# The S5 layer's scan on VectorE alone, a chunk of the prompt and one of the sample in one instruction

## The chip, the cores and the metric

One core of one Trainium2 chip runs the whole kernel. Its engines are TensorE (PE in the profile; PEld its weight loads), VectorE (DVE), ScalarE (ACT), GpSimd (POOL) and SyncE (SP), which issues most DMAs. The metric is the device time of one execution in microseconds, as the median of several runs.

## What is computed

A prompt of 1024 tokens and a sample of 512 go through two layers: latent attention, which the change leaves alone, and a bidirectional S5 state space layer. Both end in a scaled residual and a layer norm. Of the reference this is the S5 layer; the scan is a linear recurrence over the tokens, in both directions, for 64 groups of 16 channels with 64 complex states each:

```python
def _s5_scan(us, lam_bar, b_bar, c):
    bu = lax.complex(jnp.einsum('lgp,gnp->lgn', us, b_bar.real),
                     jnp.einsum('lgp,gnp->lgn', us, b_bar.imag))
    a = jnp.broadcast_to(lam_bar, bu.shape)
    _, h = lax.associative_scan(_ssm_combine, (a, bu), axis=0)
    return jnp.einsum('gpn,lgn->lgp', c, h).real

def _s5(x, w_in, ...):
    u, gate = jnp.split(x @ w_in, 2, axis=-1)
    ...
    def per_seq(us):
        y_f = _s5_scan(us, lam_bar[0], b_bar[0], c[0])
        y_b = _s5_scan(us[::-1], lam_bar[1], b_bar[1], c[1])[::-1]
        return y_f + y_b

    y = lax.map(per_seq, ug).reshape(B, L, S5_WIDTH) + d.astype(f32) * uf
    y = jax.nn.gelu(y).astype(x.dtype)
    y = y * jax.nn.sigmoid(y @ w_glu + b_glu)
    return (y * jax.nn.silu(gate)) @ w_out
```

## The kernel before

Every product of full precision is three matmuls of 512 columns (`mm3`, L89 to L91) on operands cut into a high and a low part. In the S5 layer (`s5`) the tokens go in chunks of 8: 128 chunks of the prompt and 64 of the sample, 192 places. A chunk's own contribution to the state is a matmul, the recurrence over the chunks is a scan on the vector engines, and a chunk's output comes from the state ahead of it and from its own tokens (a Toeplitz matrix), again by matmuls. Partitions are (direction, state); the backward direction is stored mirrored, so that one scan does both. `X[half]` is [128, 192 places, re | im, 32 groups]; half 0 lies in the memory zone SA, half 1 in SB.

In the order of the program:

- the product that gives u (8 blocks of 128 columns, 3 chunks of 512 tokens). When u's first half is there, `states_in(q)`, q = 0 to 7, makes half 0's states, four groups each: matmuls L1203, copies L1208 and L1209 on ScalarE, L1211 and L1212 on VectorE;
- the gate's products in 14 passes (`gate(i)`): two with all three chunks of tokens, six with the first chunk alone, six with the other two. The first two passes hold `states_in(8)` to `states_in(15)`, half 1, whose copies are all ScalarE's;
- the scan: `scan` gives the three instructions of a step of one chain, a product with the factors (L1222) and two sums (L1223). The prompt's chain runs on VectorE, the sample's on GpSimd. `begin` makes a chain ready, `advance(n)` emits n steps of each ready chain in turn. Half 0 is one chain of 32 groups; half 1 is two of 16 groups, which begin in the first and in the second gate pass;
- in the last six passes `first(i)` puts the outputs of four groups, i = 0 to 9, between the gate's products: `states_out(i)` gathers the states of four groups (L1343 on VectorE, L1344 on ScalarE, L1345 on GpSimd) into one place, which all i below 10 share with each other, `outputs(i)` makes 12 matmuls (L1359 to L1361), the gelu (L1363) and, after every second i, writes 128 rows of y (L1367);
- the gated linear unit (GLU): `load_y(m)` fetches row block m of y (L1403) into a place that the gate's weights held, GpSimd rounds it to the high part (L1406), VectorE subtracts (L1407); `load_w` does the same with weights (L1419 to L1421). `early(kt)` multiplies row block kt for the first two column blocks. The outputs 10 to 15 stand between;
- the rest of the GLU, the output projection and the norm.

The Tile layer's scheduler takes this program and settles the order on every engine by its own simulated timeline, so an engine's order differs from the program's. The scan's and the copies' code:

```python
1214    def scan(chain, c):
1216        half, lo, hi, seq = chain
1217        eng = (nc.vector, nc.gpsimd)[seq]
1218        prev, cur = (X[half][:, 128 * seq + i, :, lo:hi] for i in (c - 1, c))
1219        sh = [128, 2, 2, hi - lo]
1220        lam = k.lam[:, :, :, half * 32 + lo:half * 32 + hi]
1221        t = k.scan[half][seq][:, :, :, lo:hi]
1222        return [lambda: eng.tensor_mul(t, prev.unsqueeze(2).broadcast_to(sh), lam),
1223                lambda: eng.tensor_add(cur, cur, t[:, 0]), lambda: eng.tensor_add(cur, cur, t[:, 1])]
...
1232    def advance(n):
1234        for _ in range(n):
1235            for f in zip(*[scan(h, todo[h].pop(0)) for h in todo if todo[h]]):
1236                for g in f:
1237                    g()
...
1343        nc.vector.tensor_copy(st[0:64], xv[0:64])
1344        nc.scalar.copy(st[64:128, :, :, 0:128], xv[64:128, :, :, 127::-1])
1345        nc.gpsimd.tensor_scalar(st[64:128, :, :, 128:192], xv[64:128, :, :, 191:127:-1], 1.0, 0.0, op0=ALU.mult, op1=ALU.add)
```

In tile names, `ident` is half 0's buffer for the prompt's products (the identity is no longer needed then), `scan` the other two, `lam` the factors.

## Time and profile before

| | |
|---|---|
| median of 3 runs | 1690.88 us (1687.87 to 1691.36) |
| span of the profiled execution | 1688.0 us |
| TensorE busy | 1571.6 us, 93% |
| VectorE busy | 1177.9 us, 70% |
| GpSimd busy | 630.6 us, 37% |
| ScalarE busy | 571.1 us, 34% |

The span runs from the first instruction to the last; for the profiled execution the page has no other time. A busy share is a mean over all stages of the program, and says little of the one stage that the change is in. A matmul's end is modelled, so its price is read from the distance of one start to the next. In rows of the order of time, "x2" merges two instructions, and the square bracket gives the idle time ahead of an instruction with what ended it. The names of waits are the last releaser by the profile.

### The profile page before, as it was taken

Reading aid. Unit: us, or ns where it says so; the run is one execution under the profiler, and the core shown is the slowest. Engines: PE = TensorE matmul, PEld = TensorE weight load, DVE = VectorE, ACT = ScalarE, POOL = GpSimd, SP = SyncE. Lnnn points to the kernel's source line nnn. Section 1 sums busy time; section 2 is a strip of 40 time slices with the busy share of each in tenths; the row PEclk is TensorE's granted clock in tenths of the full one; section 3 lists DMA queues with packets and bytes.
Section 4 is the critical chain, followed back from the end, with each engine's and each line's share of the span. In section 5 each row is a group of like instructions: output and inputs, shape, how many; then the busy total and the mean of one; then the engine's idle time right before and its main releaser. Section 6 shows DMA issues by size and latency. Waiting matters only on the chain.

```text
span 1688.0 us, 23831 instructions
## 1 busy us (share of the span) xinstructions
PE 1571.6 (93%) x7932; PEld 1332.1 (79%) x7932; DVE 1177.9 (70%) x2667; ACT 571.1 (34%) x997; POOL 630.6 (37%) x1137
## 2 busy tenths in 40 slices
PE   8997777999999999999999999999877899999997
PEld 7996566887887878888888888888656788887886
DVE  5539995377766676788757742489999975553776
ACT  3442222153444444444511113416613363222000
POOL 6807673133232232344311000077798624233110
PEclk9998988999999999999999999999988999999999
DMA  5654555923223232442344426525665589564553
GB/s 172 176 158 148 168 197 159 324 67 88 77 77 102 67 98 86 148 138 80 122 150 141 125 94 177 152 49 145 195 185 163 174 260 296 187 206 142 187 143 93
DMA packets 205930, 249.68 MB, mean 148 GB/s; under 512 B 26608, under 2 KB 149104, under 8 KB 204784
## 3 DMA queue, kind: packets, MB, share of 16 engines
q1 hardware_dynamic: 197168, 232.36, 45.9%
q10 hardware_dynamic: 8640, 15.80, 2.6%
q8 instruction: 63, 1.03, 0.3%
q14 instruction: 59, 0.48, 0.1%
HBM read 155.89 MB, written 90.11 MB: 146 GB/s over the span
## 4 chain that ended last, share of the span: by engine, by line
PE 62%; DVE 26%; DMA 6%; issue 2%; POOL 2%; ACT 1%; SPq 1%; DVEq 0%; POOLq 0%; ACTq 0%
PE B L90 8%; PE B L91 8%; PE S L91 8%; PE B L89 8%; PE S L89 8%; PE S L90 8%; DVE SA L1223 4%; DVE SB L1223 4%; PE B L538 4%; DVE ident L1222 3%; DMA X<-SG 2%; DVE scan L1222 2%; PE S L504 2%; PE S L503 2%; DVE SA L1071 2%
## 5 line engine op out<-in xcount | busy, mean ns | idle before, releaser
L523 POOL TENSOR_SCALAR SC<-SC,R 128x1024 f32<-128x1024 f32 (+1 forms) x96 | 99.8, 1040 | 226.7 <-DVE R L522 189.8
L89 PE MATMUL B<-X,SB 128*128 128x512 f32 x392 | 156.7, 400 | 2.1 <-DVE SC L1125 1.5
L90 PE MATMUL B<-X,SB 128*128 128x512 f32 x392 | 154.8, 395 | 0.0
L91 PE MATMUL B<-X,SB 128*128 128x512 f32 x392 | 154.5, 394 | 0.0
L540 ACT CAST X<-B 128x512 fp32r<-128x512 f32 x160 | 89.9, 590 | 128.2 <-PE B L538 127.9
L541 DVE TENSOR_TENSOR X<-B,X 128x512 fp32r<-128x512 f32 x160 | 106.3, 684 | 23.4 <-ACT X L540 23.0
L516 ACT ACTIVATE SC<-S,R 128x1024 f32<-128x1024 f32 (+1 forms) x96 | 93.8, 977 | 66.3 <-DVE R L513 59.1
L513 DVE TENSOR_REDUCE R<-S 128x1 f32<-128x1024 f32 (+1 forms) x96 | 99.3, 1039 | 21.5 <-PE S L504 21.1
L1223 DVE TENSOR_TENSOR SB<-SB,scan 128x32 f32<-128x32 f32 x504 | 101.2, 236 | 2.1
L538 PE MATMUL B<-ident,SC 128*128 128x128 f32 x640 | 89.5, 272 | 5.9 <-POOL SC L523 5.9
L538 PEld LDWEIGHTS B<-ident,SC 128*128 128x128 f32 x640 | 76.4, 140 | 21.2 <-POOL SC L523 6.8
L89 PEld LDWEIGHTS B<-X,SB 128*128 128x128 f32 x392 | 74.8, 191 | 17.4 <-DVE SC L1125 1.7
L91 PEld LDWEIGHTS B<-X,SB 128*128 128x128 f32 x392 | 74.6, 190 | 15.6
L90 PEld LDWEIGHTS B<-X,SB 128*128 128x128 f32 x392 | 74.8, 191 | 14.8
L1223 DVE TENSOR_TENSOR SA<-SA,ident 128x64 f32<-128x64 f32 x252 | 80.9, 321 | 4.9
L89 PE MATMUL B<-X,R 128*128 128x512 f32 x192 | 78.7, 410 | 5.3 <-ACT R L1323 3.0
L90 PE MATMUL B<-X,R 128*128 128x512 f32 x192 | 76.3, 397 | 0.0
L91 PE MATMUL B<-X,R 128*128 128x512 f32 x192 | 75.6, 395 | 0.0
L89 PE MATMUL S<-SA,X 128*128 128x384 f32 (+2 forms) x208 | 69.5, 342 | 6.4 <-POOL SA L96 6.4
L90 PE MATMUL S<-SA,X 128*128 128x384 f32 (+2 forms) x208 | 70.3, 340 | 0.3 <-DVE SA L97 0.3
L91 PE MATMUL S<-SA,X 128*128 128x384 f32 (+2 forms) x208 | 69.6, 335 | 0.0
L99 POOL TENSOR_SCALAR R<-R,gq 128x64 fp32r<-128x64 f32 (+1 forms) x96 | 35.7, 383 | 89.1 <-PE B L90 45.9
(414 smaller groups left out, 4549.2 us busy)
## 6 DMA issues: line engine op xcount, KB each, us to landing
R<-WG SPq DMA_DIRECT2D x112, 128.0 KB, 3.4
R<-EU SPq DMA_DIRECT2D x52, 224.0 KB, 3.3
EU<-SA SPq DMA_DIRECT2D x16, 512.0 KB, 4.3
WO<-SA SPq DMA_DIRECT2D x8, 1024.0 KB, 4.1
WG<-X SPq DMA_DIRECT2D x16, 512.0 KB, 3.0
X<-WO SPq DMA_DIRECT2D x16, 512.0 KB, 6.2
SG<-SC ACTq DMA_DIRECT2D x24, 256.0 KB, 2.5
SC<-SG SPq DMA_DIRECT2D x24, 256.0 KB, 2.9
```

The costliest lines, as they stand in the source:

```text
L89: nc.tensor.matmul(ps, ah, bh, start=first, stop=False)
L90: nc.tensor.matmul(ps, ah, bl, start=False, stop=False)
L91: nc.tensor.matmul(ps, al, bh, start=False, stop=last)
L99: nc.gpsimd.tensor_scalar(hi, raw, g, 0.0, op0=ALU.mult, op1=ALU.add)
L513: nc.vector.reduce_max(nm, self.S[:, :L], axis=AX.X, negate=True)
L516: nc.scalar.activation(P, self.S[:, :L], AF.Exp, bias=nm, accum_out=rsum)
L523: nc.gpsimd.tensor_scalar(P, P, rsum, 0.0, op0=ALU.mult, op1=ALU.add)
L538: nc.tensor.transpose(ps[:, t, :], P[:, (t0 + t) * 128:(t0 + t + 1) * 128], self.k.ident)
L540: nc.scalar.copy(a[:, :, qsl], ps)
L541: nc.vector.tensor_sub(b[:, :, qsl], ps, a[:, :, qsl])
L1222: return [lambda: eng.tensor_mul(t, prev.unsqueeze(2).broadcast_to(sh), lam), lambda: eng.tensor_add(cur, cur, t[:, 0]), lambda: eng.tenso ...
L1223: lambda: eng.tensor_add(cur, cur, t[:, 0]), lambda: eng.tensor_add(cur, cur, t[:, 1])]
```

## The change

The scan runs on VectorE alone. For places below 64 one instruction covers chunk c of the prompt and chunk c of the sample (places c and 128 + c): a product of 128x256 and two sums of 128x128. Above 64 only the prompt is left: 128x128 and 128x64 while the other half is in turn with it, and two chains of 16 groups when a half is alone. Half 1 becomes one chain of 32 groups, which begins when all its states are emitted. `advance` is given a time in us instead of a number of steps. The mirrored copy of the sample's states goes from GpSimd to ScalarE. The product buffers are tiles of their own, and the factors are laid out by half. The size of a scratch buffer for DMAs that GpSimd describes is set; none of the kernel's DMAs is of that kind (the queues in the profile are the two hardware ones). The rest of the diff takes out comments.

```diff
-    def scan(chain, c):
-        half, lo, hi, seq = chain
-        eng = (nc.vector, nc.gpsimd)[seq]
...
-    def begin(half, lo, hi):
-        for seq, n in enumerate((128, 64)):
-            todo[half, lo, hi, seq] = list(range(2, n))
...
+    todo = [[], []]
+
+    def step(half, c, lo=0, hi=32):
+        n = hi - lo
+        if c < 64:
+            both = X[half][:, 0:192].rearrange("p (a b) r g -> p a b (r g)", b=64)[:, 0:3:2]
+            prev, cur = both[:, :, c - 1], both[:, :, c]
+            sh = [128, 2, 2, 64]
+            lam = k.lam[:, half].rearrange("p k r g -> p k (r g)").unsqueeze(1).broadcast_to(sh)
+            t = k.scan[half]
+            return [lambda: nc.vector.tensor_mul(t, prev.unsqueeze(2).broadcast_to(sh), lam),
+                    lambda: nc.vector.tensor_add(cur, cur, t[:, :, 0]), lambda: nc.vector.tensor_add(cur, cur, t[:, :, 1])]
+        prev, cur = (X[half][:, i, :, lo:hi] for i in (c - 1, c))
+        lam = k.lam[:, half, :, :, lo:hi]
+        t = k.scan[half][:, 0].rearrange("p k (r g) -> p k r g", r=2)[:, :, :, lo:hi]
+        return [lambda: nc.vector.tensor_mul(t, prev.unsqueeze(1).broadcast_to([128, 2, 2, n]), lam),
+                lambda: nc.vector.tensor_add(cur, cur, t[:, 0]), lambda: nc.vector.tensor_add(cur, cur, t[:, 1])]
+
+    def begin(half):
+        todo[half] = list(range(2, 128))
+        owed[0] = min(owed[0], 0.0)
+
+    owed = [0.0]
+
+    def advance(us):
+        owed[0] += us
+        while owed[0] > 0 and any(todo):
+            ready = [h for h in range(2) if todo[h]]
+            if len(ready) == 1 and todo[ready[0]][0] >= 64:
+                h, c = ready[0], todo[ready[0]].pop(0)
+                steps = [step(h, c, 0, 16), step(h, c, 16, 32)]
+                owed[0] -= 0.72
+            else:
+                cs = [todo[h].pop(0) for h in ready]
+                steps = [step(h, c) for h, c in zip(ready, cs)]
+                owed[0] -= 1.15 if len(ready) == 1 else sum(0.74 if c < 64 else 0.48 for c in cs)
+            for f in zip(*steps):
                 for g in f:
                     g()
...
-            advance(6)
+            advance(5.5)
...
-            if (i, kt) == (0, 6):
-                begin(1, 0, 16)
-            elif (i, kt) == (1, 6):
-                begin(1, 16, 32)
+            if (i, kt) == (1, 6):
+                begin(1)
...
-            advance(5 if i == 0 else (2, 2, 1, 1)[4 - len(cs)] if len(cs) == 3 else 1)
+            advance(0.69 * len(cs) + (1.4 if i < 2 else 0))
...
-        nc.gpsimd.tensor_scalar(st[64:128, :, :, 128:192], xv[64:128, :, :, 191:127:-1], 1.0, 0.0, op0=ALU.mult, op1=ALU.add)
+        nc.scalar.copy(st[64:128, :, :, 128:192], xv[64:128, :, :, 191:127:-1])
...
     def first(i):
-        while i == 8 and any(todo.values()):
-            advance(1)
+        if i == 8:
+            advance(1e3)
         outputs(i, states_out(i))
+        advance(1.3)
         load(i + 2)
...
-    while any(todo.values()):
-        advance(1)
+    advance(1e3)
...
-        k.scan = [(t[0], t[2]), (t[1], t[2])]
+        k.lam = const.tile([128, 2, 2, 2, G // 2], F32, name="lam")
+        k.scan = [const.tile([128, 2, 2, G], F32, name="scan%d" % i) for i in range(2)]
```

In the lines of the kernel after, a combined step is L1226 and L1227, a step of the prompt alone L1231 and L1232, the copies of the states are L1361 to L1363, the output matmuls L1377 to L1379, the subtraction for y L1425.

The order of VectorE where half 1's first step stands. Before, with half 0's own steps around it (SA is half 0, SB half 1):

```order
L1222 TENSOR_TENSOR ident<-SA,lam 128x128 [waits DVE_49]
L1223 TENSOR_TENSOR SA<-SA,ident 128x64 [waits DVE_49] x2
L1222 TENSOR_TENSOR scan_80<-SB,lam 128x4x16 [waits Activation_49]
L1222 TENSOR_TENSOR ident<-SA,lam 128x128 [waits DVE_49]
L1223 TENSOR_TENSOR SB<-SB,scan_80 128x2x16 [waits DMAHW3_49,DMAHW4_49,DMAHW2_49,DMAHW5_49,DMAHW1_49,DMAHW6_49,DMAHW0_49,DMAHW7_49,DVE_49,PE_49]
L1223 TENSOR_TENSOR SA<-SA,ident 128x64 [waits DVE_49]
```
and now:

```order
L1231 TENSOR_TENSOR scan_80<-SA,lam 128x4x16 [waits DVE_49] x2
L1232 TENSOR_TENSOR SA<-SA,scan_80 128x2x16 [waits DVE_49] x4
L1231 TENSOR_TENSOR scan_80<-SA,lam 128x4x16 [waits DVE_49] x2
L1232 TENSOR_TENSOR SA<-SA,scan_80 128x2x16 [waits DVE_49]
L1226 TENSOR_TENSOR scan_81<-SB,lam 128x256 [waits Activation_49]
L1232 TENSOR_TENSOR SA<-SA,scan_80 128x2x16 [waits DVE_49] x2
L1227 TENSOR_TENSOR SB<-SB,scan_81 128x2x64 [waits DMAHW3_49,DMAHW4_49,DMAHW2_49,DMAHW5_49,DMAHW1_49,DMAHW6_49,DMAHW0_49,DMAHW7_49,DVE_49,PE_49]
L1232 TENSOR_TENSOR SA<-SA,scan_80 128x2x16 [waits DVE_49]
```
Before, half 1's first instruction waits for ScalarE's copies of the first 16 groups, q = 8 to 11; now for those of all 32. The second sum's rows show that half 0's prompt steps go on between. Ahead of the place stand, of half 0, 62 combined steps and 26 rounds of two chains of 16; behind it 27 such rounds and 11 whole steps, in turn with 39 of half 1, up to the first L1361.

The order of TensorE at the first output product (L1359 before, L1377 now; X and R are the gate's operands in L89 to L91). Before:

```order
L1359 MATMUL B<-X_11015 128x192 x2
L1360 MATMUL B<-X_11016,X_11015 128x192
L1361 MATMUL B<-X_11016,X_11015 128x192
L1359 MATMUL B<-X_11015 128x192
L1360 MATMUL B<-X_11016,X_11015 128x192
```
and now:

```order
L1377 MATMUL B<-X_10370 128x192 x2
L89 MATMUL B<-X_88,R 128x512
L90 MATMUL B<-X_89,R 128x512
L91 MATMUL B<-X_88,R 128x512
L89 MATMUL B<-X_90,R 128x512
```
The other ten matmuls of output 0 followed its first two directly, and 30 gate matmuls stood between outputs 0 and 1. Now 60 gate matmuls stand there, and then the rest of output 0 and all of output 1 without any between; outputs 2 to 7 have 24 gate matmuls ahead of each. After the gate's last matmul come two matmuls of output 9, 24 of the GLU with y0 and y1, the rest of output 8, and 24 more with y2 and y3. Before, output 8 stood among the gate's matmuls and outputs 9 to 12 ahead of all of the GLU.

The order of VectorE at the scan's end (L1407 and L1425 are the subtractions for y, L1421 and L1439 those for the weights). Before:

```order
L1222 TENSOR_TENSOR scan_80<-SB,lam 128x4x16 [waits DVE_49]
L1223 TENSOR_TENSOR SB<-SB,scan_80 128x2x16 [waits DVE_49] x2
L1343 COPY X_12057<-SB 64x1536 [waits PE_49]
L1421 TENSOR_TENSOR X_12059<-X_12057,X_12059 128x512 [waits DMAHW3_49,PE_49,Activation_49]
L1343 COPY X_11016<-SB 64x1536 [waits PE_49]
L1421 TENSOR_TENSOR X_12059<-X_12057,X_12059 128x512 [waits DMAHW1_49,Activation_49]
L1343 COPY X_12057<-SB 64x1536 [waits DVE_49,PE_49,Pool_49]
L1343 COPY X_12057<-SB 64x1536 [waits DVE_49,PE_49]
L1407 TENSOR_TENSOR X_12059<-R,X_12059 128x1536 [waits DMAHW5_49,Pool_49]
```
and now:

```order
L1231 TENSOR_TENSOR scan_81<-SB,lam 128x4x16 [waits DVE_49]
L1425 TENSOR_TENSOR X_11474<-R,X_11474 128x1536 [waits DMAHW7_49,Pool_49]
L1231 TENSOR_TENSOR scan_81<-SB,lam 128x4x16 [waits DVE_49]
L1232 TENSOR_TENSOR SB<-SB,scan_81 128x2x16 [waits DVE_49] x2
L1439 TENSOR_TENSOR X_11473<-X_11472,X_11473 128x512 [waits DMAHW1_49,Activation_49]
L1232 TENSOR_TENSOR SB<-SB,scan_81 128x2x16 [waits DVE_49]
L1425 TENSOR_TENSOR X_11474<-R,X_11474 128x1536 [waits DMAHW0_49,Pool_49]
L1232 TENSOR_TENSOR SB<-SB,scan_81 128x2x16 [waits DVE_49]
L1361 COPY X_10371<-SB 64x1536 [waits DVE_49]
L1361 COPY X_11472<-SB 64x1536
```
The whole scan stood ahead of the first subtraction for y. Now the last steps stand behind that for y0 (the first L1425), and the copy of output 8's states, the first L1361 here, behind that for y1. On SyncE the load of y7 stood behind four loads of weights that came after the last rows of y were written; now it follows the writes, with three such loads behind it.

## Rows read from the trace of the kernel before

**Rows 1.** Order of time on PE; start us, us, line, operation, tiles [idle before]

```profile
1249.85 0.39 PE L89 MATMUL B<-X,R 128*128 128x512 f32 x1
...
1251.21 0.49 PE L1359 MATMUL B<-X 128*128 128x192 f32 x2
...
1263.16 0.98 PE L1360 MATMUL B<-X,X 128*128 128x192 f32 x2 [11.14 <-DVE scan L1222]
...
1379.26 0.48 PE L1359 MATMUL B<-X 128*128 128x192 f32 x2
...
1379.58 0.49 PE L1360 MATMUL B<-X 128*128 128x192 f32 x2
...
1454.18 0.39 PE L89 MATMUL B<-X,X 128*128 128x512 f32 x1
```

**Rows 2.** Busy time by stage; us, busy us (instructions) by engine, granted clock, DMA

```profile
core 0: us, PE busy (x) PEld busy (x) DVE busy (x) ACT busy (x) POOL busy (x), PEclk, DMA share, GB/s
1249.85:1454.18 204.33, 169.46 (x806) 149.61 (x804) 163.57 (x635) 78.18 (x82) 115.04 (x243) 0.92 0.66 206
```

**Rows 3.** Waits of PE in the stretch; us in total, times, longest

```profile
PE B L1360 <- DVE scan L1222: 19.6, 2, 11.1
...
PE B L1359 <- DMA X<-TT: 3.6, 1, 3.6
```

**Rows 4.** The copies of the states; the last row, of the line's answer: min/median/max ns

```profile
1241.79 19.81 POOL L1345 TENSOR_SCALAR X<-SA 64x512 f32<-64x512 f32 x1 [3.32 <-PE B L90]
...
1260.39 2.06 ACT L1344 COPY X<-SA 64x1024 f32<-64x1024 f32 x1 [17.90 <-DVE SA L1223]
...
L1343 DVE COPY X<-SA x8: 1445/1552/2475, 1260.4 to 1355.3; 64x1536 f32<-64x1536 f32 x8
```

**Rows 5.** Order of time on DVE, half 0's steps beside GpSimd's

```profile
1102.50 0.43 DVE L1222 TENSOR_TENSOR ident<-SA,lam 128x128 f32<-128x128 f32 x1
...
1103.84 0.43 DVE L1222 TENSOR_TENSOR ident<-SA,lam 128x128 f32<-128x128 f32 x1
```

**Rows 6.** The same, GpSimd without work

```profile
1146.52 0.29 DVE L1222 TENSOR_TENSOR ident<-SA,lam 128x128 f32<-128x128 f32 x1
...
1147.36 0.29 DVE L1222 TENSOR_TENSOR ident<-SA,lam 128x128 f32<-128x128 f32 x1
```

**Rows 7.** The same, three chains in turn

```profile
1248.80 0.22 DVE L1222 TENSOR_TENSOR scan<-SB,lam 128x64 f32<-128x64 f32 x1
1248.93 0.29 DVE L1222 TENSOR_TENSOR ident<-SA,lam 128x128 f32<-128x128 f32 x1
1249.13 0.22 DVE L1222 TENSOR_TENSOR scan<-SB,lam 128x64 f32<-128x64 f32 x1
```

**Rows 8.** The same, half 1's two chains alone

```profile
1298.25 0.54 DVE L1223 TENSOR_TENSOR SB<-SB,scan 128x32 f32<-128x32 f32 x4
...
1298.98 0.54 DVE L1223 TENSOR_TENSOR SB<-SB,scan 128x32 f32<-128x32 f32 x4
```

**Rows 9.** Order of time on ACT, the last states of half 1

```profile
1209.78 1.05 ACT L1211 COPY SB<-S 64x508 f32<-64x508 f32 x1
1210.63 0.64 ACT L1212 COPY SB<-S 64x252 f32<-64x252 f32 x1
```

**Rows 10.** The eight loads of y, L1403

```profile
DMA to landing us min/median/max: 4.5/6.3/7.3
```

**Rows 11.** The way of y7: gelu, load, rounding, subtraction

```profile
1423.68 0.49 ACT L1363 ACTIVATE X<-B 128x384 f32<-128x384 f32 x1 [1.46 <-PE B L1361]
...
1434.19 0.34 SPq L1403 DMA_DIRECT2D R<-Y  x1
...
1440.21 0.43 SPq L1403 DMA_DIRECT2D R<-Y  x1
...
1446.94 1.48 POOL L1406 TENSOR_SCALAR X<-R 128x1536 fp32r<-128x1536 f32 x1 [4.98 <-DMA R<-Y]
...
1448.46 1.76 DVE L1407 TENSOR_TENSOR X<-R,X 128x1536 fp32r<-128x1536 f32 x1 [3.27 <-POOL X L1406]
```

More of the change, by code (lines that the diff above doesn't have):

```diff
@@ L1009, in prep_a @@
         for r in range(2):
-            nc.gpsimd.tensor_copy(lam[:, r, r], pr[:, 8, :])
-            nc.gpsimd.tensor_scalar(lam[:, 1 - r, r], pi[:, 8, :], (1.0, -1.0)[r], 0.0, op0=ALU.mult, op1=ALU.add)
+            halves = [x[:, 8, :].rearrange("p (h g) -> p h g", h=2) for x in (pr, pi)]
+            nc.gpsimd.tensor_copy(lam[:, :, r, r], halves[0])
+            nc.gpsimd.tensor_scalar(lam[:, :, 1 - r, r], halves[1], (1.0, -1.0)[r], 0.0, op0=ALU.mult, op1=ALU.add)
         self.pb = [self.t("pbr", [128, T, G]), self.t("pbi", [128, T, G])]
@@ L1212, in states_in @@
             cp(x[64:128, :, :, 129:192], v[64:128, :, :, 191:128:-1])
-    def scan(chain, c):
-        half, lo, hi, seq = chain
-        eng = (nc.vector, nc.gpsimd)[seq]
-        prev, cur = (X[half][:, 128 * seq + i, :, lo:hi] for i in (c - 1, c))
-        sh = [128, 2, 2, hi - lo]
-        lam = k.lam[:, :, :, half * 32 + lo:half * 32 + hi]
-        t = k.scan[half][seq][:, :, :, lo:hi]
-        return [lambda: eng.tensor_mul(t, prev.unsqueeze(2).broadcast_to(sh), lam),
-                lambda: eng.tensor_add(cur, cur, t[:, 0]), lambda: eng.tensor_add(cur, cur, t[:, 1])]
@@ L1225, in s5 @@
-    todo = {}
-    def begin(half, lo, hi):
-        for seq, n in enumerate((128, 64)):
-            todo[half, lo, hi, seq] = list(range(2, n))
-    def advance(n):
-        for _ in range(n):
-            for f in zip(*[scan(h, todo[h].pop(0)) for h in todo if todo[h]]):
+    todo = [[], []]
[14 more added lines that the diff above has]
+                lambda: nc.vector.tensor_add(cur, cur, t[:, 0]), lambda: nc.vector.tensor_add(cur, cur, t[:, 1])]
@@ L1271, in s5 @@
                     if q == 7:
-                        begin(0, 0, 32)
+                        begin(0)
             ps = ahead.get((m, c))
@@ L1581, in trunk @@
             setattr(k, n, const.tile(shape, F32, name=n))
-        k.lam = const.tile([128, 2, 2, G], F32, name="lam")
-        t = [k.ident] + [const.tile([128, 128], F32, name="scan%d" % i) for i in range(2)]
-        t = [x.rearrange("p (k r g) -> p k r g", k=2, r=2) for x in t]
-        k.scan = [(t[0], t[2]), (t[1], t[2])]
+        k.lam = const.tile([128, 2, 2, 2, G // 2], F32, name="lam")
+        k.scan = [const.tile([128, 2, 2, G], F32, name="scan%d" % i) for i in range(2)]
         k.bcol = const.tile([128, 8], F32, name="bcol")
@@ L1647 @@
     from concourse.bass_utils import run_bass_kernel_spmd
-    nc = bacc.Bacc("TRN2", target_bir_lowering=False, num_devices=1)
+    nc = bacc.Bacc("TRN2", target_bir_lowering=False, num_devices=1, dynamic_dma_scratch_size=1024)
     ins = arrays(inputs)
```

## The prediction

> **What bounds the kernel now.** I read the busy times by stage first, then TensorE's waits, then VectorE's order of time in the scan, then the way of y into the gated linear unit (GLU). Everything before 1101 us stays as it is: the scan starts there, and the order of TensorE up to its first output product is the same in both kernels. From there I compare one stretch, between two matmuls that both orders have: from 1249.85 us, seven matmuls ahead of the first output product, to the first product with y7 at 1454.18 us; after it the two orders of TensorE are equal again. In this stretch the order has 420 matmuls of 512 columns and 192 output matmuls, in both kernels. A 512-column matmul takes 0.227 us (six from 1249.85 to 1251.21), an output matmul 0.325 us; the trace shows it as two instructions [rows 1]. So the work is 420 x 0.2268 + 192 x 0.325 = 157.7 us, and the stretch lasts 204.3 us, of which TensorE is busy 169.5 [rows 2]. It loses 46.6 us: 34.9 us idle and 11.8 us in running slower than those two prices, at a granted clock of 0.92 in the mean [rows 2], so part of the time at the lower of its two levels, 1.2 GHz instead of 2.4. This is all that the change can win here.
>
> Who causes the idle time: the output products wait 19.6 us in two waits, 11.1 the longest, each for a VectorE instruction of the scan, and 3.6 us for a load of the Toeplitz matrices [rows 3]. The longest ends at 1263.16 [rows 1]: the states of the first four groups could be copied only when half 0's scan was done, which ScalarE's copy had awaited until 1260.39 [rows 4]. So VectorE's scan bounds this stretch, and TensorE's products are its victims.
>
> **What a scan step costs on VectorE.** Beside GpSimd's sample chain a step of half 0 (a 128x128 product, two 128x64 sums) repeats every 1.34 us [rows 5]. The same step without GpSimd at work repeats every 0.84 us [rows 6]; each of its three instructions waits for the one before. With three chains in turn nothing waits: a 128x64 product gives way to the next after 0.13 us, a 128x128 after 0.20 [rows 7], so 64 more columns cost 0.067 us. Two chains of 16 groups in turn need 0.73 us a round [rows 8].
>
> The combined step (product 128x256, sums 128x128) is in no row. Lower bound: no more than today's solo step, 0.84. Upper bound: the sample's step as a second full step behind it, 1.68. I take 0.84 plus four times 0.067 (two blocks of 64 columns in the product, one in each sum) = 1.11 us alone, and 0.34 + 2 x 0.20 = 0.74 us beside another chain, since rows 7 already show that columns cost their count and no more. A prompt-only step of 32 groups beside another chain is 0.20 + 2 x 0.13 = 0.47.
>
> **Half 0.** 62 combined steps, 68.8 us, then 26 split rounds, 18.9: from 1101.4 to about 1189. Then VectorE meets the first instruction of half 1 in its queue, which waits for ScalarE; the other 38 prompt steps of half 0 are queued behind it. ScalarE's last copy of half 1's states ends at 1211.3 [rows 9]; so VectorE stands still some 22 us. Before, the first of two half-1 chains could begin earlier. Behind it: 39 half-1 steps at 0.74, 27 split rounds at 0.67, 11 steps at 0.47 = 52.1 us, half 0 done at 1263.4. That is 3 us later than today's, not earlier.
>
> **Outputs 0 to 7.** What is won comes from the order on TensorE: ahead of output 0 stand 60 more gate matmuls (13.6 us), which today come after it. TensorE reaches output 0 at 1249.85 + 0.65 + 13.6 = 1264.1. The states' copies then take VectorE 1.55 us and ScalarE 2.06 [rows 4]; the wait is about 2 us where 11.1 stood. Output 1 follows with nothing between, and its states have the same place: ScalarE copies 2.06 and now also the sample's 64x512, bounded by the nearest copy, 64x508 in 1.05 [rows 9], so TensorE waits 3.3 us. The six after that have 24 gate matmuls each ahead (5.4 us) against 3.1 us on ScalarE and, on VectorE, 7 solo steps (7.8 us) and a copy against 9.3 us: no wait, but hardly any slack. Up to the gate's end the order has 252 gate matmuls and 100 output matmuls: 1249.85 + 57.2 + 32.5 + 5.3 = 1344.8, and a few us more of slow running, against 1379.26 today [rows 1].
>
> **From the gate's end G to y7.** Now something else is late. The place of y0's rows is freed only at G. A load of y lands in 6.3 us [rows 10], GpSimd rounds it in 1.48, VectorE subtracts in 1.76 [rows 11]: with the handovers 9.9 us. The order has 24 products with y0 and y1 ahead of output 8, and the last scan steps of VectorE stand behind y0's subtraction: TensorE idles about 9.4 us. y2's rows come into the place of y0's, so y2 is ready some 10.3 us behind y0, and TensorE has 5.4 + 3.2 us of products until then: 1.7 us; output 11's load, as today, 3.6 [rows 3]. y6 and y7: from an output's gelu, the rows are stored, read back, rounded and subtracted. Today this took from 1424.2 to 1450.2 us, 26 us, and the load went out only at 1440.2, behind four weight loads; the load of another row block ahead of them went out at 1434.2 [rows 11]. The change moves them behind y7's load, which saves up to these 6 us: 20. TensorE has 78 products, 17.7 us, after output 15: I count the difference, some 2.5 us, for y6 and y7 together (both ends: nothing, if the queue is empty; 8.3 us, if all stays as today).
>
> **The sum.** Idle: 2 + 3.3 + 9.4 + 1.7 + 3.6 + 2.5 = 22.5 us instead of 34.9. Slow running in proportion, 11.8 x 22.5/34.9 = 7.6. Loss 30.1 instead of 46.6: **16.5 us** won. The profiled span of 1688.0 becomes 1671.5. The median of the runs, 1690.88, stands 2.9 us above the span, so I say 1674. GpSimd's own work goes at no cost elsewhere: its scan and copies had nothing behind them that TensorE waits for, except the clash with VectorE, which is in the 1.34 against 0.84.
>
> GpSimd's mirrored copy at 1241.79 took 19.81 us [rows 4], and within this time VectorE's instructions kept their distances of 0.13 and 0.20 us [rows 7]: the copy starved, not VectorE. The Trainium skill ("SBUF — State Buffer", section "SBUF: two separate sides") says that the two engines' shared port pair is an exclusive lock, held for the whole instruction by whoever comes first. By that rule moving eight copies of 1.1 us off GpSimd would free VectorE of 9 us more before output 7, and the sum would be 9 us better. The trace disagrees at this copy, though the step's 1.34 against 0.84 shows the clash in the other direction.
>
> **Rivals.**
> 1. *VectorE becomes the bound (slower).* It is busy 163.6 of the stretch's 204.3 us today [rows 2], and takes over all that GpSimd did in the scan. If a combined step costs x more than my 1.11 (two pieces of memory in one operand), the first 62x hide in the 22 us of standing still, up to x = 0.36; the 39 steps before output 0 and the 23 between outputs do not: 62x. The gain is gone at x = 0.27, and it is slower by over 0.2% from 0.32, a step of 1.43 us; at the bound 1.68 the time would be 1674 + 35 + 13 = 1722. For it: no row has such an operand. Against it: VectorE's states' copy reads 1536 scattered elements in 1.55 us at the median [rows 4], so scattered columns cost no more. The Trainium skill ("Perfetto Trace Analysis", section "Optimizing Scalar/DVE Operations") advises to take work off a saturated VectorE, even to GpSimd, though it doubts that between these two. The trace bears out the doubt.
> 2. *The tail of y stays as slow as today (smaller gain).* 26 us against 17.7 us of products: 8.3 us idle instead of 2.5, and the slow running after it, 8 us in all: 1682. For it: the queue of DMAs is as full. Against it: the weight loads go behind.
> 3. *TensorE is covered better (larger gain).* If y0's load lands in 4.5 us, the shortest of the eight [rows 10], output 0 and the tail don't wait: idle 12, slow 4, loss 16: 30 us won, 1660.
> 4. *Nothing is won.* Half 0 isn't done earlier, and TensorE loses at GLU what it wins before: 1690. This needs 35 us of idle time again, 12 us more than the rows give.
>
> **Chances.** Forecast 0.61 (1665 to 1682); rival 1 0.11, of which 0.10 over 0.2% slower; rival 2 0.13; rival 3 0.09; rival 4 0.06. About 0.2%, 3.4 us, is what a measurement of this kernel tells from no change: faster 0.83, same 0.07, slower 0.10. Range 1658 to 1688: it takes in rivals 2 and 3 and leaves out the others.
>
> **What the profile would show.** Right: combined steps every 1.11 us from 1101; VectorE idle some 20 us before 1211, ended by ScalarE; output 0's wait near 2 us at 1264 to 1267; the gate ending near 1346; one wait near 9 us for y0 then. Wrong: steps over 1.3 us; half 0 done after 1275; waits of over 3 us at outputs 2 to 7; over 6 us idle ahead of y6 or y7.

## The result, and the profile after

| | before | after |
|---|---|---|
| median of the runs | 1688.04 us (5 runs, 1687.31 to 1691.36) | 1676.96 us (5 runs, 1674.56 to 1681.59) |
| ratio | | 0.9932, 95% interval 0.9915 to 0.9950 |
| span of the profiled execution | 1688.0 us | 1675.1 us |

The change wins 11.1 us at the medians and 12.9 us between the two profiled executions. The forecast was 16.5 us.

The stretch of the prediction, from the first output product (1249.54) to the first product with y7 (now 1443.19), by the windows view; from 1353.90 on TensorE waits for y0. It answers to [rows 2] and holds the same number of matmul instructions (806).

```profile
core 0: us, PE busy (x) PEld busy (x) DVE busy (x) ACT busy (x) POOL busy (x), PEclk, DMA share, GB/s
1249.54:1353.90 104.36, 96.71 (x453) 82.34 (x452) 89.41 (x481) 50.35 (x53) 0.00 (x0) 0.97 0.70 210
1353.90:1443.19 89.29, 72.12 (x353) 62.36 (x353) 41.89 (x82) 36.30 (x40) 17.28 (x10) 0.92 0.70 226
1249.54:1443.19 193.65, 168.83 (x806) 144.70 (x805) 131.30 (x563) 86.64 (x93) 17.28 (x10) 0.95 0.70 217
```

The stretch is 193.65 us long instead of 204.33. TensorE is idle for 24.8 us of it (34.9 before) and runs slow for 168.83 - 157.66 = 11.2 us (157.66 is the work at full price that the prediction gives as 157.7; 11.8 before). VectorE is busy 131.3 us instead of 163.6, although it does GpSimd's part too. So the stretch wins 10.7 us. Behind it, from y7 to the end, the execution is 1.9 us shorter (TensorE was idle there for 1.6 us before and is not now), and ahead of it 0.3 us.

What TensorE waits for in the stretch, by the waits view (us in total, times, longest); beside [rows 3]:

```profile
PE S L89 <- POOL X L1424: 11.7, 1, 11.7
PE B L1378 <- ACT X L1363: 3.5, 1, 3.5
PE B L1378 <- DMA X<-WO: 1.8, 1, 1.8
PE B L1378 <- ACT X L1362: 1.8, 1, 1.8
PE B L1377 <- ACT X L1381: 1.4, 1, 1.4
PE B L1377 <- ACT R L1341: 1.1, 1, 1.1
```

The 19.6 us for the scan are gone. Instead there is one wait of 11.7 us for y0, and small ones for ScalarE's copies of the states. In TensorE's order of time the waits stand here (the bracket is the idle time ahead), beside [rows 1]:

```profile
1268.28 1.01 PE L1378 MATMUL B<-X,X 128*128 128x192 f32 x2 [1.76 <-ACT X L1362]
...
1276.84 0.59 PE L1378 MATMUL B<-X 128*128 128x192 f32 x2 [3.50 <-ACT X L1363]
...
1351.17 0.39 PE L91 MATMUL B<-X,R 128*128 128x512 f32 x1
...
1353.27 0.59 PE L1377 MATMUL B<-X 128*128 128x192 f32 x2 [1.12 <-ACT R L1341]
1365.55 0.80 PE L89 MATMUL S<-X 128*128 128x512 f32 x1 [11.68 <-POOL X L1424]
```

Output 0 waits 1.8 us where 11.1 stood, output 1 3.5; the gate's last product is at 1351.17 instead of 1379.03 (the output product behind it stands in [rows 1]); then comes y0's wait.

VectorE's order of time: two combined steps at the scan's start, beside [rows 5], and the standstill in front of half 1, with the end of half 0.

```profile
1100.68 0.43 DVE L1226 TENSOR_TENSOR scan<-SA,lam 128x256 f32<-128x256 f32 x1
1101.14 0.62 DVE L1227 TENSOR_TENSOR SA<-SA,scan 128x128 f32<-128x128 f32 x2
1101.79 0.42 DVE L1226 TENSOR_TENSOR scan<-SA,lam 128x256 f32<-128x256 f32 x1
...
1211.47 0.42 DVE L1226 TENSOR_TENSOR scan<-SB,lam 128x256 f32<-128x256 f32 x1 [23.28 <-ACT SB L1213]
...
1264.23 1.53 DVE L1361 COPY X<-SA 64x1536 f32<-64x1536 f32 x1
...
1371.30 1.54 DVE L1361 COPY X<-SB 64x1536 f32<-64x1536 f32 x1
```

A combined step takes 1.11 us. VectorE stands still 23.3 us, half 0 is done at 1264.2, and the first states of half 1 are copied only at 1371.3, when the whole scan is over. That this copy stands so late was in the order listed with the change, but the prediction did not ask what it costs; the experiments turn on it.

### The profile page after: what moved, and what is told of

Same layout as the page of the kernel before. It is cut to its first block, busy times and chain, and to the rows that moved or that the text cites. A ratio compares the mean times of both kernels' runs of the same rounds, so it can differ in the third digit from the quotient of the medians.

```text
span 1675.1 us, 23206 instructions
## 1 busy us (share of the span) xinstructions
PE 1574.3 (94%) x7932; PEld 1330.7 (79%) x7932; DVE 1121.1 (67%) x2640; ACT 581.4 (35%) x1009; POOL 415.4 (25%) x563
## 4 chain that ended last, share of the span: by engine, by line
PE 72%; DVE 14%; DMA 8%; ACT 2%; issue 2%; POOL 1%; SPq 1%; DVEq 0%; ACTq 0%; POOLq 0%
PE B L89 11%; PE B L90 11%; PE B L91 11%; PE S L91 9%; PE S L89 9%; PE S L90 9%; PE B L538 4%; DVE SA L1072 2%; PE S L1204 2%; PE S L504 2%; PE S L503 2%; DVE SA L1070 2%; DVE R L1071 2%; DVE SA L1227 1%; DMA R<-WG 1%
## 5 line engine op out<-in xcount | busy, mean ns | idle before, releaser
L89 PE MATMUL B<-X,SB 128*128 128x512 f32 x392 | 156.6, 399 | 2.4 <-DVE SC L1126 1.5
L91 PE MATMUL B<-X,SB 128*128 128x512 f32 x392 | 154.3, 394 | 0.0
L89 PEld LDWEIGHTS B<-X,SB 128*128 128x128 f32 x392 | 74.9, 191 | 17.7 <-DVE SC L1126 1.7
L91 PEld LDWEIGHTS B<-X,SB 128*128 128x128 f32 x392 | 74.5, 190 | 15.6
L89 PE MATMUL B<-X,R 128*128 128x512 f32 x192 | 79.0, 412 | 5.7 <-ACT R L1341 3.0
L91 PE MATMUL B<-X,R 128*128 128x512 f32 x192 | 76.3, 398 | 0.0
L89 PE MATMUL S<-SA,X 128*128 128x384 f32 (+2 forms) x208 | 70.4, 344 | 5.5 <-POOL SA L96 5.5
L91 PE MATMUL S<-SA,X 128*128 128x384 f32 (+2 forms) x208 | 69.9, 337 | 0.0
L90 PE MATMUL B<-X,X 128*128 128x512 f32 x168 | 68.2, 406 | 0.3 <-DVE X L541 0.2
L89 PE MATMUL B<-X,X 128*128 128x512 f32 x168 | 67.3, 401 | 0.0
L91 PE MATMUL B<-X,X 128*128 128x512 f32 x168 | 66.2, 394 | 0.0
```

The lines of the kernel that those rows point to most:

```text
L89: nc.tensor.matmul(ps, ah, bh, start=first, stop=False)
L90: nc.tensor.matmul(ps, ah, bl, start=False, stop=False)
L91: nc.tensor.matmul(ps, al, bh, start=False, stop=last)
```

## The experiments

Two questions: why y0's wait is there, and which part of the change earns the gain. Every run was compared with the kernel before on the same chip; the medians:

| kernel | median us | ratio, 95% interval |
|---|---|---|
| the change | 1676.96 | 0.9932 (0.9915 to 0.9950) |
| y0_piece | 1675.76 | 0.9922 (0.9903 to 0.9941) |
| copy_on_gpsimd | 1678.38 | 0.9935 (0.9917 to 0.9953) |
| before_copy_on_scalar | 1685.18 | 0.9974 (0.9962 to 0.9986) |
| before_scan_on_vector | 1667.91 | 0.9888 (0.9866 to 0.9911) |
| scan_only | 1672.31 | 0.9914 (0.9898 to 0.9929) |
| unmerged | 1676.47 | 0.9929 (0.9915 to 0.9943) |
| late_begin | 1673.41 | 0.9901 (0.9883 to 0.9919) |
| copies_on_vector | 1672.31 | 0.9906 (0.9889 to 0.9924) |
| scan_and_copies_on_vector | 1680.66 | 0.9951 (0.9936 to 0.9967) |
| scan_and_two_copies_on_vector | 1669.03 | 0.9878 (0.9860 to 0.9896) |
| unmerged_one_chain | 1685.22 | 0.9975 (0.9966 to 0.9985) |

**y0's place.** The rows of y0 get a place of their own, cut off from those that the gate's results pass through, so that their load need not wait until the gate's last result is stored.

```diff
-    ry = Region(k, "R", (13, F32))
+    ry = Region(k, "R", (6, F32), (7, F32))
```

> The changed kernel, with the place of y0's rows cut off from the places that the gate's results pass through. Theory: in the changed kernel y0's load goes out only at 1359.1 us because its place is one piece with that of the gate's last result, whose store to memory must land first; with a piece of its own the load needs only the gate's last matmul (1351.4) and goes out near 1354, TensorE's wait for y0 falls from 11.7 us to about 7, and the time by 4 to 6 us, to about 1672. Rival: the wait is set by the weights' load or by VectorE's scan steps ahead of y0's subtraction, and the time stays at 1677 within 2 us.

Not so: 1675.76 us, which can't be told from the change. SyncE's and GpSimd's order of time, first of the change, then of this kernel:

```profile
1359.11 0.79 SPq L1421 DMA_DIRECT2D R<-Y  x2
...
1364.02 4.59 POOL L1424 TENSOR_SCALAR X<-R 128x1536 fp32r<-128x1536 f32 x2 [217.26 <-DMA R<-Y]
```

```profile
1355.45 3.86 SPq L1421 DMA_DIRECT2D R<-Y  x2
...
1362.46 3.00 POOL L1424 TENSOR_SCALAR X<-R 128x1536 fp32r<-128x1536 f32 x2 [213.74 <-DMA R<-Y]
...
1367.98 0.80 PE L90 MATMUL S<-X 128*128 128x512 f32 x1 [3.20 <-DVE X L1425]
...
1355.00:1364.00 9.00, 0.01 (x1) 0.01 (x1) 7.05 (x44) 0.62 (x1) 1.48 (x2) 0.55 0.97 353
```

The load goes out 3.7 us earlier and its rounding starts only 1.6 us earlier: the DMA engines are 97% busy in these 9 us (last row, the windows view). The wait for y0's high part shrinks by 1.0 us, but the one for its low part, VectorE's subtraction, grows from 1.0 to 3.2: scan steps stand ahead of the subtraction on VectorE, and it starts only at 1366.2. So the rival holds. The place alone is not the bound; behind it stand the load, which shares the DMA engines with the output's and the GLU's weights, and VectorE's scan.

**The copy back on GpSimd.** The change, but with the mirrored copy of the sample's states where it was.

```diff
-        nc.scalar.copy(st[64:128, :, :, 128:192], xv[64:128, :, :, 191:127:-1])
+        nc.gpsimd.tensor_scalar(st[64:128, :, :, 128:192], xv[64:128, :, :, 191:127:-1], 1.0, 0.0, op0=ALU.mult, op1=ALU.add)
```

> The changed kernel, with the copy of the sample's mirrored states back on GpSimd: one part undone. Theory: beside VectorE steps that wait for each other the copy takes 1.1 to 2.7 us and runs next to ScalarE's, so the wait ahead of output 1 falls from 3.5 us to about 2.4 and the time by 0 to 2 us. Rival 1: where VectorE's split rounds leave no gap the copy starves as the one of 19.8 us did, outputs 4 to 8 wait 5 us or more each, and the time is above 1690. Rival 2, by the rule of the exclusive port pair: each copy stops VectorE for 1.1 us, 16 copies, 1 to 3 us slower.

1678.38 us: no difference from the change. Output 1 waits 2.7 us instead of 3.5, and other waits take up the rest.

**The copy alone.** The kernel before, with only this line the other way round (copy on ScalarE, sample's scan still on GpSimd).

> The kernel before, with only the copy of the sample's mirrored states moved from GpSimd to ScalarE: one part alone. Theory: the starved copy of 19.8 us ended before VectorE's own copy, so it delayed nothing; the time stays within 3 us of 1688. Rival, by the rule of the exclusive port pair: VectorE gains 8 copies of 1.1 us ahead of output 7 and the time falls by about 9 us, to 1679.

1685.18 us, 3.5 less than before: about the theory's 3, and far from the rival's 9. TensorE's waits and the stretch by windows:

```profile
PE B L1360 <- ACT X L1344: 30.2, 1, 30.2
...
1247.42:1449.33 201.91, 163.99 (x805) 144.71 (x805) 156.07 (x684) 91.86 (x97) 65.60 (x185) 0.92 0.67 209
```

The order came out differently: one wait of 30.2 us at output 0 instead of the waits of 11, 8, 5 and 3 us. TensorE is idle for longer than before (201.91 - 163.99 = 37.9 us instead of 34.9), but runs slow for only 163.99 - 157.7 = 6.3 us instead of 11.8. So slow running does not follow the idle time. And since the order changed too, the copy's effect is not seen by itself.

**The scan's engine and the copy, nothing merged.** The kernel before with two lines changed; the sample's chain is now one more chain on VectorE, in turn with the prompt's, and half 1 stays two chains of 16 groups.

```diff
-        eng = (nc.vector, nc.gpsimd)[seq]
+        eng = nc.vector
...
-        nc.gpsimd.tensor_scalar(st[64:128, :, :, 128:192], xv[64:128, :, :, 191:127:-1], 1.0, 0.0, op0=ALU.mult, op1=ALU.add)
+        nc.scalar.copy(st[64:128, :, :, 128:192], xv[64:128, :, :, 191:127:-1])
```

> The kernel before, with the scan's sample chains on VectorE but as instructions of their own, half 1 still in two chains that begin early, and the copy on ScalarE: the change without merging. Theory: what pays is that GpSimd no longer slows VectorE (1.34 against 0.84 us a step) and what the new order on TensorE hides; two chains in turn fill each other's waits, so half 0 costs 0.94 us for a step of prompt and sample against 1.115 merged; half 0 done near 1265 us, the time 1670 to 1682, no slower than the changed kernel. Rival: merging is what makes the scan fit on VectorE; without it VectorE has some 42 us more to issue, ends the scan later than 1385 us, and the time is 1700 or more.

1667.91 us: the change's own idea in two lines, 2 us below the theory's range, and faster than the change by 9 us at the medians, 7 by the ratios; the two intervals don't touch. VectorE's order of time: a step of half 0, the two standstills, the states of half 1; and the copies of half 0's states, of the line's answer.

```profile
1101.83 0.29 DVE L1222 TENSOR_TENSOR ident<-SA,lam 128x128 f32<-128x128 f32 x1
1102.04 0.29 DVE L1222 TENSOR_TENSOR scan<-SA,lam 128x128 f32<-128x128 f32 x1
...
1102.78 0.28 DVE L1222 TENSOR_TENSOR ident<-SA,lam 128x128 f32<-128x128 f32 x1
...
1176.94 0.23 DVE L1222 TENSOR_TENSOR scan<-SB,lam 128x64 f32<-128x64 f32 x1 [11.07 <-ACT SB L1211]
...
1211.26 0.23 DVE L1222 TENSOR_TENSOR scan<-SB,lam 128x64 f32<-128x64 f32 x1 [4.51 <-ACT SB L1211]
...
1343.88 1.55 DVE L1343 COPY X<-SB 64x1536 f32<-64x1536 f32 x1
...
1373.13 0.42 DVE L1223 TENSOR_TENSOR SB<-SB,scan 128x32 f32<-128x32 f32 x2
...
L1343 DVE COPY X<-SA x8: 1446/1539/1556, 1270.6 to 1331.9; 64x1536 f32<-64x1536 f32 x8
```

Four things are seen. Six small instructions, two chains in turn, take 0.95 us for the same work as the merged step's three in 1.11: nothing waits for the instruction before it. The first chain of half 1 begins at 1176.9, 34.5 us before half 1 begins in the change. The scan's end, 1373.5, is no earlier than the change's, but states of half 1 are copied from 1343.9 on: its first 16 groups are done long before the others. So outputs 8 to 11 can stand ahead of y0, and y0's wait is gone. And half 0 is not done sooner: its first copy is 10 us later than before (1260.4, [rows 4]), but the eight follow one another faster, and the last is at 1331.9 instead of 1355.3. What TensorE waits for there:

```profile
PE B L1360 <- DVE SB L1223: 10.9, 2, 7.4
PE B L1360 <- ACT X L1344: 3.5, 1, 3.5
PE B L1359 <- DMA X<-TT: 2.3, 1, 2.3
```

**The scan's engine alone.** As above with the copy left on GpSimd.

> The kernel before with one line changed: all chains of the scan on VectorE; the mirrored copy of the sample's states stays on GpSimd, nothing is merged. Together with the runs that moved the copy alone (1685.2) and both (1667.9) this gives the parts of the gain. Theory (the scan's two engines taking turns at memory is what cost): nearly all of the 20 us comes from the scan: 1668 to 1673 us, with waits of at most a few us for the GpSimd copy. Rival (the GpSimd copy, starved by a VectorE that now never pauses, needs some 20 us for each of eight blocks): TensorE waits for it at output 0 and again at outputs 1 to 7, 1680 us or more.

1672.31 us: the theory. Of the 20 us between before and the unmerged kernel some 16 come with the scan's engine; the copy's 4 more are at the edge of what these intervals tell apart. The scheduler settles a new order for each of these kernels, so the 16 us are those of the engine together with the order that follows; no run holds the order fixed. GpSimd's copies and VectorE's sums in their order of time:

```profile
1241.83 29.83 POOL L1345 TENSOR_SCALAR X<-SA 64x512 f32<-64x512 f32 x1 [93.05 <-DVE ident L1222]
...
1296.54 1.18 POOL L1345 TENSOR_SCALAR X<-SA 64x512 f32<-64x512 f32 x1 [6.58 <-PE B L1361]
...
1295.40 0.48 DVE L1223 TENSOR_TENSOR SB<-SB,scan 128x32 f32<-128x32 f32 x4
...
1296.42 1.45 DVE L1223 TENSOR_TENSOR SB<-SB,scan 128x32 f32<-128x32 f32 x4
```

The first copy starves for 29.8 us, as in [rows 4]. The other seven of half 0 do not: each takes some 1.1 to 2.6 us, and VectorE's instructions beside it lose about 1 us (here 0.48 becomes 1.45).

**The change without its merged instruction.** Loops, turns and the one chain of half 1 as in the change.

```diff
-                steps = [step(h, c) for h, c in zip(ready, cs)]
+                steps = [step(h, c, seq=q) for h, c in zip(ready, cs) for q in range(2 if c < 64 else 1)]
```

> The changed kernel with its loop structure kept, but the sample's step again as three instructions of its own, taking turns with the prompt's (no 128x256 product). The scheduler answers by finishing half 0 ahead of half 1's chain, so that output 0 comes some 180 matmuls earlier; 26 products stand ahead of output 8's last ten matmuls, as in the change. Theory 1 (the merged step, 1.115 us against 0.95 for two chains in turn, is not what costs the 9 us; the cover of y0 is): half 0 done 10 us or more earlier, but y0's wait stays at 9 to 12 us and the time stays within 3 us of 1677. Rival (62 steps of 0.165 us, 10 us of VectorE's time, are what the merged form costs): 1666 to 1670 us.

1676.47 us, as theory 1 had it. VectorE's and TensorE's order of time:

```profile
1246.85 1.56 DVE L1353 COPY X<-SA 64x1536 f32<-64x1536 f32 x1
...
1359.73 0.80 PE L89 MATMUL S<-X 128*128 128x512 f32 x1 [11.77 <-POOL X L1416]
```

The step takes 0.95 us and the order gives half 0 the turn; its states are copied 17 us earlier, output 0 waits for nothing, and none of it arrives: y0's wait is 11.8 us, and a later row block of y waits 3.2.

**Outputs ahead of y0.** Two ways to put more outputs there without touching the chains: half 1's chain begun later in the program, and three mirrored copies moved to VectorE.

```diff
-            if (i, kt) == (1, 6):
+            if (i, kt) == (2, 0):
```

> The changed kernel with half 1's chain begun ten loop turns later in the program. The scheduler then leaves TensorE's order as it is up to the gate's end, but puts all 12 matmuls of output 8 ahead of the first products with y0 (in the change 2 of them), and 22 more behind the first 24 products instead of 10. Theory (the change loses its last 9 us at the gate's end, because nothing covers the way of y0): the ten output matmuls are worth 3.3 us, the wait for y0 falls from 11.7 to about 8 us, the time is 1672 to 1674 us. Rival A (what costs is VectorE standing still 23 us for half 1's states): that stays at 20 us or more, and the time stays at 1677 within 2 us. Rival B: the copies of output 8's states now stand ahead of y0's subtraction on VectorE and the wait only moves there: 1677 or more.

```diff
-            cp = nc.vector.tensor_copy if q < 8 else nc.scalar.copy
+            cp = nc.vector.tensor_copy if q < 8 or q > 12 else nc.scalar.copy
```

> The changed kernel with the mirrored copies of the last three state blocks of half 1 on VectorE instead of ScalarE (blocks 13 to 15). The scheduler answers with 22 output matmuls ahead of the first product with y0 and 12 more behind a single product, where the change has 2, then 24 products, then 10. Theory (y0 uncovered): 20 output matmuls more are 6.5 us, the wait for y0 falls from 11.7 to 5 us or less, and the time is 1669 to 1673 us. Rival: VectorE is in the gate's end the late one, its scan now ends later by three copies of some 2 us, the outputs ahead of y0 wait for it instead, and the time is 1676 to 1682.

1673.41 and 1672.31 us, both in the range of the theory, with intervals that just overlap the change's. The longest waits of TensorE, of the first kernel and then of the second:

```profile
1370.06 1.01 PE L1378 MATMUL B<-X,X 128*128 128x192 f32 x2 [9.50 <-ACT X L1362]
```

```profile
1274.80 1.01 PE L1378 MATMUL B<-X,X 128*128 128x192 f32 x2 [10.16 <-ACT X L1362]
```

y0's wait is gone in both, and another stands in its place. In the first, output 8 waits for the states that the scan gives at its very end (1360.6 to 1370.1): rival B in kind, though the time is the theory's. In the second, half 1's states can be copied from 1353.2 on, 18 us earlier than in the change, but half 0's only from 1272.9 on, 9 us later, and output 0 waits. VectorE can put its work early at one end or at the other. (The first one's profiled execution stood above its median, at a span of 1680.0; only where the waits are is taken from it.)

**More copies on VectorE.** The fast unmerged kernel with the edit of `copies_on_vector`, for three and for two blocks.

> The kernel before with the scan's chains all on VectorE and unmerged, the mirrored copy on ScalarE, and besides the mirrored copies of half 1's last three state blocks on VectorE. Theory (with the scan on one engine and the way of y0 covered by outputs, what is left are single waits for the states' copies of outputs 0, 1 and 8 to 11): the 3.5 us of ScalarE's copy at the gate's end go, the rest stays: 1664 to 1667 us. Rival (VectorE is the bound now, so three copies of some 2 us more on it make the waits for the scan longer): output 0 waits 10 us instead of 7.4, and the time is 1670 us or more.

> The same with only the last two blocks' copies on VectorE (14 and 15). The order then puts 29 output matmuls in a row behind 14 products, and output 12's last ones late. Theory: between 1667.9 (no copies moved) and the run with three: 1664 to 1669 us. Rival as there: 1670 us or more.

Three blocks: 1680.66 us, the rival; output 0 waits 13.6 us instead of 7.4. Two: 1669.03 us, not to be told from 1667.91, although output 0 waits 12.9 us there. So that wait is not what the third block costs. In the trace with three, waits of 4.7 us for a rounding of the GLU's weights and of 3.6 us in two for y's subtractions stand besides, which with two are 0.5 us and nothing; why they come was not tried.

**One chain in the fast kernel.** The test of the last reading: only half 1's two chains become one of 32 groups.

```diff
-            if (i, kt) == (0, 6):
-                begin(1, 0, 16)
-            elif (i, kt) == (1, 6):
-                begin(1, 16, 32)
+            if (i, kt) == (1, 6):
+                begin(1, 0, 32)
```

> The fastest kernel so far (the kernel before with the scan's chains unmerged on VectorE and the copy on ScalarE, 1667.9 us), with one thing of the change put in: half 1 as one chain of 32 groups that begins when all its states are there, instead of two of 16 that begin one after the other. Nothing is merged. TensorE's order then has, behind the gate, 2 output matmuls and 48 products before the next output, where the fast kernel has 48 output matmuls first. Theory (the one chain is what costs the change 9 us: no state of half 1 is ready until the whole chain is, so nothing stands ahead of y0): VectorE stands still once, over 20 us, TensorE waits 9 to 12 us for y0, and the time is 1674 to 1680 us. Rival (the merged instruction is what costs): it stays at 1666 to 1670 us.

1685.22 us: the theory in its direction and in its place, and 5 us beyond its range. Its longest waits, on VectorE and on TensorE:

```profile
1211.04 0.29 DVE L1222 TENSOR_TENSOR scan<-SB,lam 128x128 f32<-128x128 f32 x1 [19.27 <-ACT SB L1211]
...
1268.51 1.55 DVE L1341 COPY X<-SA 64x1536 f32<-64x1536 f32 x1 [9.35 <-PE B L1359]
```

```profile
1359.62 0.80 PE L89 MATMUL S<-X 128*128 128x512 f32 x1 [11.66 <-POOL X L1404]
...
1371.33 0.73 PE L89 MATMUL S<-SA,X 128*128 128x512 f32 x2 [2.08 <-POOL SA L1404]
1374.91 0.79 PE L90 MATMUL S<-SA,X 128*128 128x512 f32 x1 [2.85 <-DVE SA L1405]
```

With one chain the long standstill and y0's wait of 11.7 us are back, and with them 17 us at the medians, 15 by the ratios. Why this is more than what the change loses was not tried. Two things are seen that the change doesn't have. Half 1's last steps are of 32 groups, 0.84 us each, where the change splits them into two chains, 0.73. And VectorE stands still a second time, 9.3 us ahead of the copy of output 1's states, whose place TensorE has not given back. (The profiled execution is the longest of the twelve; only where the waits are is taken from it.)

## Why the prediction was right, and where its terms were off

The sign, the range and the mechanism held: waits of outputs 0 to 7 are covered by the new order, and y0 waits in their place. 1674 was said, 1677 came, but this is nearer than the working deserves. The gain was 11.1 us instead of 16.5. The five runs of the kernel before have a median 2.8 us below the three that the forecast started from, and 2.2 us were won outside the stretch, for which the prediction had no reason: that is luck. The terms, one by one, from one execution of each kernel:

| term | forecast | measured |
|---|---|---|
| combined step alone | 1.11 us | 1.11 |
| VectorE stands still | 22 us | 23.3 |
| half 0 done | 1263.4 | 1264.2 |
| wait at output 0, at output 1 | 2 and 3.3 us | 1.8 and 3.5 |
| waits at outputs 2 to 7 | none | none |
| the gate's end | near 1346 | 1351.6 |
| y0's wait | 9.4 us | 11.7 |
| y2's wait | 1.7 us | 1.1 |
| output 11's load, y6 and y7 | 3.6 and 2.5 us | 1.8 and 0 |
| idle in the stretch | 22.5 us | 24.8 |
| slow running | 7.6 us | 11.2 |
| won in the stretch | 16.5 us | 10.7 |
| won outside of it | none | 2.2 |

- **The step on VectorE** was the boldest price, since no row had the operand, and it was exact: 0.84 for the dependent instructions plus 64-column blocks at 0.067. Rival 1 needed 1.38 and more, and fell with it. Beside half 0's split rounds a combined step and a round came every 1.42 us (1211.47 to 1212.89), where the prediction's 0.74 and 0.67 make 1.41; no row ahead of it showed the 0.67. (Two slips change no term: the stretch begins six matmuls ahead of the first output product and not seven, and half 0's first two counts make 87.8 us and not 87.7.)
- **Slow running** was the term that was mis-sized most: it was taken in proportion to the idle time. The windows view shows that it does not go by that. Behind output 0's wait of 1.8 us the clock is at its lower level, behind output 1's 3.5 us it is 0.72 over 6 us, and behind y0's it is at the lower level again. The last row is of y0_piece, behind output 0's wait of 1.74 us there: the clock stays at its upper level.

```profile
1268.00:1271.00 3.00, 2.72 (x8) 2.72 (x9) 2.33 (x7) 1.51 (x2) 0.00 (x0) 0.51 0.09 32
...
1277.00:1283.00 6.00, 6.00 (x27) 5.92 (x28) 2.91 (x7) 1.39 (x3) 0.00 (x0) 0.72 0.26 77
...
1365.00:1369.00 4.00, 2.46 (x5) 1.66 (x6) 3.48 (x5) 0.62 (x1) 3.54 (x2) 0.50 0.05 17
...
1267.70:1270.70 3.00, 2.71 (x17) 2.71 (x18) 2.73 (x9) 2.01 (x3) 0.00 (x0) 1.00 0.12 44
```

  Behind the wait of 1.8 us the five distances from 1268.28 to 1271.55 are 3.27 us where 5 x 0.325 would do: 1.6 us lost. Worked out the same way, it is 1.8 us behind output 1's wait of 3.5, 2.1 behind y0's of 11.7, 1.8 behind the 11.1 of before and 2.4 behind the 30.2 of the copy alone. A wait's length does not give the loss: in the traces of all these kernels every wait of 3.6 us and more lost 1.5 to 3.2 us, but of the 32 from 1.7 to 3.5 us 18 lost 1.5 us or more and 14 lost 0.7 or less (waits with under 1 us of work between them taken as one). Four waits of before lost 9.3 of its 11.8 us. Three of the change lost 5.6 of its 11.2; the rest, 5.6 us in small pieces, is not explained. So idle fell by 10.1 us and slow running by 0.6.
- **y0's wait** had the right place and was 2.3 us short, which is what is left of larger errors of either sign. The prediction let the load go out at the gate's end; it goes out at 1359.1, nearly 8 us after the gate's last product began. But from there to the rounding it is 4.9 us and not 6.3 and more, and the first product waits for the rounding alone: the subtraction, which the prediction put ahead of it, ends a wait of 1.0 us of its own. y0_piece shows that an earlier place is worth 1 us of this wait and nothing in the time. Output 11's load and y6/y7 were 4.3 us too high; rival 2 fell, y7 is covered.
- **Rivals 3 and 4** didn't come: y0's load is quick once it is out, but it goes out late; and half 0 isn't done earlier, as rival 4 had it, but the gate's gain isn't all given back.
- **The rule on the shared port.** I had the trace speak against it from one copy of 19.8 us, during which VectorE kept its distances. That left out the copy's end: VectorE's copy that starts at 1260.4 beside it is the one of 2.48 us in [rows 4], 0.9 more than the median, so at its end VectorE did wait for it. The Trainium skill ("SBUF — State Buffer", section "SBUF: two separate sides") lets whoever starts first hold the port pair for its whole instruction. The other seven copies of scan_only agree with it: each stops an instruction of VectorE for about the 1.1 us that a copy takes. Why the first one starves while the others get their turn, the rows don't show; in copy_on_gpsimd the first one, at 1243.7, takes 1.27 us. As to the time, the rule's 9 us are not seen: the copy back on GpSimd changes nothing in the change, and is worth at most some 4 us beside the unmerged chains.

What the prediction did not ask is whether the merged form is the best form of the change. It isn't. Taking the scan off GpSimd, with the order that the scheduler then settles, is what earns: 16 us in scan_only, 20 with the copy. Half 1 as one chain then gives part of it back (unmerged_one_chain), because none of half 1's states is ready before all are, and nothing is left to stand ahead of y0. Merging the instructions itself changes nothing that can be measured in the change's own loops (unmerged), though its step is 0.16 us longer than two chains in turn; part of half 0's 62 steps' 10 us goes into the standstill, which ends with half 1's states whatever the step costs.

## What to carry to other kernels

Before making the instructions of a dependent chain wider, try a second chain in turn with it: the wider step cost 1.11 us here, two narrow ones in turn 0.95, since each hides the other's gaps. And a scan that finishes its parts one after the other lets its consumers begin before it ends. When a wait is removed, look for the next thing on the path that has no cover, and ask which work could be ready by then; a gain in the middle (half 0 done 17 us earlier in unmerged) is worth nothing while the same thing is late at the end. And don't take slow running in proportion to idle time: a wait here was followed by 1.5 to 3.2 us of loss or by next to none, and two waits of the same length could differ in this.

## What the runs showed of the hardware that I had not expected

- VectorE and GpSimd take turns by whole instructions also where they are long. In the change's order of time on VectorE, behind y0's subtraction, a 128x64 product that takes 0.22 us elsewhere takes 1.48, as long as the rounding on GpSimd (1.48 us, [rows 11]) that runs beside it:

```profile
1365.53 1.76 DVE L1425 TENSOR_TENSOR X<-R,X 128x1536 fp32r<-128x1536 f32 x1 [2.34 <-POOL X L1424]
1367.20 1.48 DVE L1231 TENSOR_TENSOR scan<-SB,lam 128x64 f32<-128x64 f32 x1
```

  GpSimd's two roundings from 1364.02 take 4.59 us instead of 2 x 1.48; the 1.63 us more are about the subtraction's 1.76. That fits the rule named above, whichever of the two starts first.
- A GpSimd copy that comes while VectorE's instructions follow one another without a gap can starve for 19.8 us (before) or 29.8 us (scan_only), where 1.1 us is its length in later places.
- The clock fell to its lower level (0.51 granted in the 3 us behind) after an idle time of TensorE of 1.76 us, and stayed at the upper one (1.00) after 1.74 us at the same place in y0_piece and after 3.14 us in the kernel before.
